# SwiGLU by block products: three pairs in units 1 to 7 instead of two, six pairs in each of two passes of the last product, and SiLU as one ScalarE step

## The chip, the cores and the metric

The kernel is one program on one core of a Trainium2 chip. The core has five engines that run side by side: TensorE (PE in the profile; its weight loads are listed as PEld), VectorE (DVE), ScalarE (ACT), GpSimd (POOL) and SyncE (SP), which here only issues DMAs. The metric is the device time of one execution in microseconds; lower is better.

## What is computed

The reference is one transformer block on 256 tokens of width 2048, all in fp32. A conditioning vector gives six modulation vectors (`w_ada`), a mixing sublayer of three branches follows, and then a SwiGLU feed-forward part, which is the part that matters here:

```
def swiglu(h, w_ffn_in, w_ffn_out):
    gate, up = jnp.split(h @ w_ffn_in, 2, axis=-1)
    return (jax.nn.silu(gate) * up) @ w_ffn_out

h = rms_norm(x, norm2_gain[l]) * (1 + scale2) + shift2
x = x + gate2 * swiglu(h, w_ffn_in[l], w_ffn_out[l])
```

`h` is 256 x 2048, `w_ffn_in` is 2048 x 11264 (gate and up, 5632 columns each), `w_ffn_out` is 5632 x 2048. The results must come out at fp32 quality.

## The kernel before

**Products in three parts.** TensorE multiplies in fp32r. Each fp32 operand is split into a high part (the value rounded to fp32r) and a low part (the remainder), and a product is three matmuls: high by high, high by low, low by high (`mm3`, lines 158 to 161). The stationary operand is a 128x128 block of the transposed activations, the moving one 128 rows x 512 columns of weights; the sum goes into a PSUM bank of 128 x 512. There are eight banks in two pools of four, `acc` and `misc`.

**Weights.** A DMA on SyncE's queue brings 2 blocks of 128 x 512 into a buffer `raw` (four of these, 512 KB each). ScalarE casts it to `whi`, VectorE subtracts `whi` from `raw` into `wlo`. There are four buffers of each, and I call one `whi` with its `wlo` a slot. In `load_weights` these are lines 153 and 154, in `load_pair` lines 1266 and 1267. A slot can be cast again only when TensorE has read it for the last time, and a `raw` buffer can be loaded again only when its last reader on VectorE or ScalarE is done. All engines, and SyncE's queue, work strictly in order. The order on each engine is set when the program is built, by a scheduler that goes by priorities; loads and evictions run at raised priority.

**SwiGLU, first product.** 5632 columns are 11 units (`i` of 0 to 10) of 512 gate and 512 up columns. A plain unit is 16 blocks of the contraction x 2 row halves (tokens 0 to 127 and 128 to 255) x 2 column blocks x 3 matmuls, 192 in all. Units 1 to 7 go through `fast_unit`. It takes the contraction in eight pairs of blocks (`PAIRS`), and a pair with the two row halves and two column blocks (gate and up) is a 2x2 by 2x2 product of blocks. A plain pair does its 8 block products, 24 matmuls, and needs two slots. A pair marked 1 is done by seven block products (Strassen's scheme in Winograd's form), 21 matmuls: VectorE forms four sums of weight blocks (line 1270, into the buffers `OD` and `KD`), the weights then fill four slots (one of them half), and four sums of activation blocks (`sums_of_h2`) are made once, in unit 0. Products that are needed in more than one output go into four banks of the other pool; after the last such pair VectorE adds them up (line 1294: four steps that form the combinations, and four that add them into the unit's own banks, while plain pairs still run). Pairs 6 and 7 are fast, in the order 0, 1, **6**, 2, **7**, 3, 4, 5.

After a unit ScalarE takes the sigmoid of the gate half (line 1361), VectorE multiplies by the gate (line 1362) and by the up half (line 1373), and behind the first pair of the next unit TensorE transposes the result (line 1110: eight transposes), which is split into high and low parts (lines 186, 187).

**A background task.** The modulation vector `gate2` is computed on VectorE in pieces placed by `tick` between the other work (line 283: 32 steps of one weight block times one scalar; loads into `AR0`, `AR1`, `KC`). It starts at unit 8 and ends in the first pass of the last product with four bias rows (line 966) and eight short steps that go from ScalarE (line 975) to VectorE (976) to TensorE (980, 981) through one buffer `T6`; `flush` places whatever is left.

**SwiGLU, last product.** Four passes `n` of 512 output columns, each 44 blocks of the contraction x 2 row halves x 3 matmuls. Each pass ends with `add_out` (times `gate2`, plus the residual, store). In the last pass the final 14 blocks are loaded ahead and the row halves run one after the other, so that little is left behind the last matmul.

Of the kernel before, what the change touches and what calls it, by code (L numbers as in the profile page):

```python
# [71 lines left out]
def trunk(ctx: ExitStack, tc: tile.TileContext, I, out):  # L72
# [15 lines left out]
    def S(tag, shape, dtype=F32):  # L88
        return slot.tile(shape, dtype, tag=tag, name=nm(tag))
# [1090 lines left out]
    def norm2_turn(t, xs):  # L1180
        c = slice(t * P, (t + 1) * P)
        banks = []
        for j in range(KC // 4):
            ps = misc_bank([P, 4, P])
            for i in range(4):
                k = 4 * j + i
                nc.tensor.transpose(ps[:, i, :], xs[:, k * P : (k + 1) * P], ident)
            banks.append(ps)
        for j, ps in enumerate(banks):
            hf = S(f"T6", [P, 4, P]) if (j, t) == (3, 0) else scr([P, 4, P])  # L1190
            if j == 3:
                h2_raw.append(hf)
# [9 lines left out]
    h2_raw = []  # L1202
# [38 lines left out]
    def sums_of_h2():  # L1241

        sf = S("KC", [P, 4, 2, P])
        (a0, b0), (a1, b1) = ((h[:, 0:4:2, :], h[:, 1:4:2, :]) for h in h2_raw)
        for dst, x, y, op in (
            (0, a1, b1, ALU.add), (2, a0, a1, ALU.subtract), (1, sf[:, 0], a0, ALU.subtract), (3, b0, sf[:, 1], ALU.subtract)
        ):
            nc.vector.tensor_tensor(sf[:, dst], x, y, op=op)
        hi, lo = S("OS1", [P, 4, 2, P], F32R), S("OS2", [P, 4, 2, P], F32R)
        nc.scalar.copy(hi, sf)  # L1250
        nc.vector.tensor_tensor(lo, sf, hi.bitcast(F32), op=ALU.subtract)
        return hi, lo

    def load_pair(p, c0, c1, fast):


        def raw_at(c):
            raw = wp.tile([P, 2, NB], F32, tag="raw", name=nm("raw"))
            nc.sync.dma_start(raw, w_ff[2 * p * P : (2 * p + 2) * P, c : c + NB].rearrange("(k p) c -> p k c", p=P))
            return raw  # L1260

        def split(src):
# [8 lines left out]
        with prio():  # L1271
            if not fast:
                return [split(raw_at(c0)), split(raw_at(c1))]
            r0, r1 = raw_at(c0), raw_at(c1)
            b11, b21 = split(r0)
            ta, tb = S("OD", [P, 2, NB]), S("KD", [P, 2, NB])
# [9 lines left out]
    def fast_unit(i):  # L1286


        own, other = (misc_bank, acc_bank) if i % 2 else (acc_bank, misc_bank)
        ws = [load_pair(p, i * NB, DFF + i * NB, fast) for p, fast in PAIRS]  # L1290
        o = [[own([P, NB]) for _ in range(NT)] for _ in range(2)]
        shared = []
        last_fast = max(n for n, (_, fast) in enumerate(PAIRS) if fast)
        add = lambda dst, x, y: nc.vector.tensor_tensor(dst, x, y, op=ALU.add)
        for n, ((p, fast), w) in enumerate(zip(PAIRS, ws)):
            tick(2 * state["rate"])
            if n == 1 and later:
                with tc.issue_after(state["mm"].ins), prio():
                    later.pop()()
            if n == last_fast + 2:  # L1300
                with prio():
                    add(o[0][0], o[0][0], first)
                    add(o[1][0], o[1][0], u[:, 1])
            if n == last_fast + 3:
                with prio():
                    add(o[0][1], o[0][1], third)
                    add(o[1][1], o[1][1], u[:, 0])
            begun, merged = n > 0, n > last_fast
            if fast:
                if not shared:  # L1310
                    shared = [other([P, NB]) for _ in range(4)]
                    p1, p5, p7, p6 = shared
                    begun = False
                else:
                    begun = True
                s = [(h2s[0][:, j, p - 6, :], h2s[1][:, j, p - 6, :]) for j in range(4)]
                a, b = 2 * p, 2 * p + 1
                lefts = (h2_at(a, 0), h2_at(b, 0), s[3], s[0], s[2], s[1], h2_at(b, 1))
                for dst, (h, l), (wh, wl) in zip((p1, o[0][0], o[1][0], p5, p7, p6, o[0][1]), lefts, w):
                    mine = dst in shared  # L1320
                    mm3(dst, h, l, wh, wl, mine and not begun, n == last_fast, False)
            else:
                for c in range(2):
                    for t in range(NT):
                        for k in range(2):
                            h, l = h2_at(2 * p + k, t)
                            mm3(o[c][t], h, l, *w[c][k], not begun and k == 0,
                                k == 1 and (n == len(PAIRS) - 1 or n > last_fast or (c, t) == (1, 1) and n == last_fast - 1), n > last_fast)
            if n == last_fast:
                with prio():  # L1330
                    u, first, third = S("KC", [P, 2, NB]), S("T6", [P, NB]), scr([P, NB])
                    nc.scalar.copy(first, p1)
                    add(u[:, 0], p6, first)
                    add(u[:, 1], p5, u[:, 0])
                    add(third, p7, u[:, 0])
                    add(u[:, 0], p5, third)
        return o

    state["rate"] = RATE_FFN
    ring["tags"] = ("AR0", "AR1", "KC")  # L1340
    act = []
    for i in range(NFF):
# [11 lines left out]
                block(pg, h2_at, None, 0, KC, 0, w=w, tiles=(t,), steps=None if t else {N2_AT[1]: lambda: norm2_turn(1, xs)})  # L1354
        else:
            block(pg, h2_at, w_ff, 0, KC, i * NB)
        sgs = []
        with prio():
            for t in range(NT):
                sg = scr([P, NB])  # L1360
                nc.scalar.activation(sg, pg[t], AF.Sigmoid)
                nc.vector.tensor_mul(sg, sg, pg[t])
                sgs.append(sg)
        if i == 0:
            h2s = sums_of_h2()
# [31 lines left out]
    KF = 4 * NFF  # L1397
    CUT = KF - 14
    w_fo = I["w_ffn_out"]
    for n in range(4):  # L1400
        pss = [acc_bank() for _ in range(NT)]
        if n == 3:

            block(pss, act_at, w_fo, 0, CUT, n * NB, more=True)
            w = load_weights(w_fo, CUT, KF, n * NB, spare=[f"H{j}" for j in range(2, 8)])
            block(pss, act_at, None, CUT, KF, 0, w=w, tiles=(0,), go_on=True)
            with prio():
                add_out(n, 0, pss[0])

            block(pss, act_at, None, CUT, KF - LASTK, 0, w=w, tiles=(1,), go_on=True, more=True)  # L1410
            side = acc_bank()
            for cols, ps in ((slice(0, NB - LASTC), pss[1][:, : NB - LASTC]), (slice(NB - LASTC, NB), side[:, :LASTC])):
                for k in range(KF - LASTK, KF):
                    wh, wl = w[k - CUT]
                    h, l = act_at(k, 1)
                    mm3(ps, h, l, wh[:, cols], wl[:, cols], k == KF - LASTK and cols.start > 0, k == KF - 1)
                if cols.start == 0:
                    add_out(n, 1, pss[1], end=NB - LASTC)
                    add_out(n, 1, pss[1], NB - LASTC, store=False)
            add_out(n, 1, side, NB - LASTC, base=NB - LASTC)  # L1420
        else:
            if n == 0:
                state["rate"] = RATE_OUT
            block(pss, act_at, w_fo, 0, KF, n * NB)
            if n == 0:
                flush()
                gate2 = state["gate2"]
            with prio():
                for t in range(NT):
                    add_out(n, t, pss[t])  # L1430


_INS = ["x", "c", "w_ada", "b_ada", "norm1_gain", "norm2_gain", "w_in", "sb_q_gain", "sb_k_gain", "dil_q_gain",
# [23 lines left out]
```

## Time and profile before

| | |
|---|---|
| median of 3 runs | 1604.01 us (1603.54 to 1604.73) |
| the profiled execution | 1603.22 us, of which 1601.4 us span from the first to the last instruction |
| granted TensorE clock | 1.00 in that execution |
| first product, units 0 to 10 | about 882 to 1359 us of the span |
| last product | about 1359 to 1601 us |

The profile gives busy time per engine, tables of busy time by stretch of the span, groups of instructions by line, a list of instructions in order of time, a chain of work that ended last, and the waits with what ended each. An instruction's row has its start, its duration and, in brackets, the idle time ahead of it on its engine with what ended that. A row with xN merges N instructions that followed each other.

### The profile page before, as it was taken

What the parts mean: (1) busy time and instruction counts of PE and PEld (TensorE: products, weight loads), DVE (VectorE), ACT (ScalarE), POOL (GpSimd) and SP (SyncE); (2) the same over time, 40 slices, a digit from 0 to 9 for tenths busy, and PEclk for the clock granted to TensorE, in tenths of its full rate; (3) what the DMA queues carried; (4) which work ended last, traced back from release to release, by engine and by line L of the source; (5) the groups of instructions that cost most, each with busy time, mean ns of one, the idle gap of its engine ahead of it and who ended that gap; (6) DMA issues with size and microseconds to landing.
All of it is one profiled execution on the core that took longest, in us unless ns stands there. A gap on an engine that the chain in (4) does not pass through costs nothing.

```text
span 1601.4 us, 20082 instructions
## 1 busy us (share of the span) xinstructions
PE 1589.3 (99%) x7308; PEld 1314.7 (82%) x7308; DVE 1207.8 (75%) x1417; ACT 814.6 (51%) x1155; POOL 5.3 (0%) x14
## 2 busy tenths in 40 slices
PE   8999999999999999999999999999999999999998
PEld 7878888888888888888887888888888888878887
DVE  6889996888877787878657688888887777474453
ACT  5654449775754434444446555555544444444332
POOL 1000000000000000000000000000000000000000
PEclk9999999999999999999999999999999999999999
DMA  9999997668778899898666566655567799666663
GB/s 332 361 327 323 331 305 246 214 184 261 247 254 288 300 302 309 300 312 299 224 192 194 167 194 194 197 193 182 189 209 235 260 313 307 224 209 193 202 206 110
DMA packets 194595, 395.96 MB, mean 247 GB/s; under 512 B 12914, under 2 KB 27928, under 8 KB 194496
## 3 DMA queue, kind: packets, MB, share of 16 engines
q1 hardware_dynamic: 194096, 394.60, 74.9%
q8 instruction: 57, 0.93, 0.2%
q14 instruction: 42, 0.34, 0.1%
q10 hardware_dynamic: 176, 0.07, 0.0%
q0 software_dynamic: 224, 0.01, 0.0%
HBM read 392.53 MB, written 2.10 MB: 246 GB/s over the span
## 4 chain that ended last, share of the span: by engine, by line
PE 90%; DVE 3%; ACT 3%; DMA 3%; issue 1%; SPq 0%; ACTq 0%; DVEq 0%
PE acc L161 24%; PE acc L160 24%; PE acc L159 24%; PE misc L159 4%; PE misc L161 4%; PE misc L160 4%; DVE wlo L154 1%; DMA raw<-w_in 1%; ACT whi L153 1%; PE acc L429 1%; PE misc L795 1%; PE misc L1110 1%; ACT scr L624 1%; DMA A<-x 0%; DMA raw<-w_br_gla 0%
## 5 line engine op out<-in xcount | busy, mean ns | idle before, releaser
L154 DVE TENSOR_TENSOR wlo<-raw,whi 128x1024 fp32r<-128x1024 f32 (+1 forms) x434 | 514.4, 1191 | 280.3 <-ACT whi L153 278.2
L153 ACT CAST whi<-raw 128x1024 fp32r<-128x1024 f32 (+1 forms) x434 | 444.0, 1026 | 529.1 <-PE acc L161 384.2
L159 PE MATMUL acc<-whi,H 128*128 128x512 f32 x1292 | 505.7, 392 | 1.4 <-ACT H L441 0.8
L160 PE MATMUL acc<-wlo,H 128*128 128x512 f32 x1292 | 504.6, 391 | 0.8 <-DVE wlo L154 0.7
L161 PE MATMUL acc<-whi,H 128*128 128x512 f32 x1292 | 503.5, 390 | 0.4 <-DVE H L448 0.4
L161 PEld LDWEIGHTS acc<-whi,H 128*128 128x128 f32 x1292 | 242.4, 188 | 52.3 <-DVE H L448 1.6
L159 PEld LDWEIGHTS acc<-whi,H 128*128 128x128 f32 x1292 | 242.5, 188 | 52.0 <-ACT H L441 1.3
L160 PEld LDWEIGHTS acc<-wlo,H 128*128 128x128 f32 x1292 | 242.7, 188 | 50.7 <-DVE wlo L154 1.7
L1266 ACT CAST whi<-raw 128x1024 fp32r<-128x1024 f32 x112 | 109.9, 998 | 86.6 <-PE acc L161 37.4
L1267 DVE TENSOR_TENSOR wlo<-raw,whi 128x1024 fp32r<-128x1024 f32 x112 | 125.8, 1155 | 12.4 <-ACT whi L1266 12.1
L160 PE MATMUL acc<-wlo,A 128*128 128x512 f32 x312 | 121.6, 390 | 0.4 <-DVE wlo L154 0.4
L159 PE MATMUL acc<-whi,A 128*128 128x512 f32 x312 | 122.0, 391 | 0.0
L161 PE MATMUL acc<-whi,A 128*128 128x512 f32 x280 | 109.1, 390 | 0.0
L159 PE MATMUL misc<-whi,H 128*128 128x512 f32 x214 | 83.6, 391 | 0.0
L161 PE MATMUL misc<-whi,H 128*128 128x512 f32 x214 | 83.3, 389 | 0.0
L160 PE MATMUL misc<-wlo,H 128*128 128x512 f32 x214 | 83.3, 389 | 0.0
L283 DVE SCALAR_TENSOR_TENSOR ada<-AR,csil,ada 128x1024 f32<-128x1024 f32 x59 | 74.9, 1280 | 3.5 <-DMA AR<-w_ada 3.4
L160 PEld LDWEIGHTS acc<-wlo,A 128*128 128x128 f32 x312 | 58.6, 188 | 12.6 <-DVE wlo L154 0.8
L159 PEld LDWEIGHTS acc<-whi,A 128*128 128x128 f32 x312 | 58.6, 188 | 11.8
L161 PEld LDWEIGHTS acc<-whi,A 128*128 128x128 f32 x280 | 52.6, 188 | 10.6
L161 PE MATMUL acc<-whi,OS 128*128 128x512 f32 x142 | 55.3, 389 | 0.0
L161 PEld LDWEIGHTS misc<-whi,H 128*128 128x128 f32 x214 | 40.2, 188 | 8.4
(396 smaller groups left out, 1761.4 us busy)
## 6 DMA issues: line engine op xcount, KB each, us to landing
raw<-w_in SPq DMA_DIRECT2D x205, 512.0 KB, 5.1
raw<-w_ffn_in SPq DMA_DIRECT2D x176, 512.0 KB, 4.4
raw<-w_ffn_out SPq DMA_DIRECT2D x88, 512.0 KB, 4.6
AR<-w_ada SPq DMA_DIRECT2D x79, 512.0 KB, 5.0
raw<-w_out SPq DMA_DIRECT2D x32, 512.0 KB, 3.8
KC<-w_ada SPq DMA_DIRECT2D x30, 512.0 KB, 5.2
OS<-w_ada SPq DMA_DIRECT2D x16, 512.0 KB, 6.4
KD<-w_ada SPq DMA_DIRECT2D x16, 512.0 KB, 4.7
```

Of the source, the lines that this page charges most:

```text
L153: state["cast"] = nc.scalar.copy(hi[:, :n, :], raw[:, :n, :])
L154: state["split"] = nc.vector.tensor_tensor(lo[:, :n, :], raw[:, :n, :], hi[:, :n, :].bitcast(F32), op=ALU.subtract)
L159: nc.tensor.matmul(ps, lh, rh, start=start, stop=False, skip_group_check=seeded)
L160: nc.tensor.matmul(ps, lh, rl, start=False, stop=False, skip_group_check=seeded)
L161: state["mm"] = nc.tensor.matmul(ps, ll, rh, start=False, stop=stop, skip_group_check=seeded)
L283: nc.vector.scalar_tensor_tensor(acc, raw, c, acc, op0=ALU.mult, op1=ALU.add)
L429: state["warm"] = nc.tensor.matmul(ps, ones_r, wide, start=True, stop=True)
L624: nc.scalar.activation(junk, heads(b)[:, t, h, :], AF.Square, accum_out=ss[:, t, i : i + 1])
L795: nc.tensor.matmul(ps[:n, t * N_GLA + h, :].rearrange("p (s l) -> p s l", l=L), at(f, h, t)[:, :n], odd(at(f, h, t)), start=True, stop=True,)
L1110: nc.tensor.transpose(ps[:, i, :], src[:, i * P : (i + 1) * P], ident)
L1266: nc.scalar.copy(hi[:, :n, :], src)
L1267: state["split"] = nc.vector.tensor_tensor(lo[:, :n, :], src, hi[:, :n, :].bitcast(F32), op=ALU.subtract)
```

## The change

1. `PAIRS`: in units 1 to 7 pairs 5, 6 and 7 are fast, in the order 0, 1, **5**, 2, **6**, **7**, 3, 4. The merge of the shared products, formerly before the seventh and eighth pair, comes before the eighth pair and after it. `sums_of_h2` makes the activation sums of pair 5 as well (kept in `AR0`) and stands before the first SiLU.
2. The last product goes through the same function in two passes of two column blocks each. Pass A (columns 0 to 1023) has 22 pairs: 7 plain, then six times a fast and a plain one, then 3 plain. Pass B (columns 1024 to 2047) has two plain pairs and six times a fast and a plain one; the remaining 16 blocks then run as before, one column block after the other. The fast pairs are those of units 4, 5 and 6 (pairs 8 to 13); their activation sums are made in pass A from high plus low part (`sums_of_unit`, before pairs 1, 2 and 4 of the order), in `AR0`, `AR1` and `H2` to `H7`. Weight sums use `AR0` and `AR1`. In pass A the loads are issued three pairs ahead (`LOOK`), and the background task must be finished before the first fast pair (`hooks[7] = flush`).
3. Sigmoid and the multiplication by the gate become one `Silu` on ScalarE.

```
-RATE_OUT = 2.0
+RATE_OUT = 2.5
+LOOK = 3
-PAIRS = ((0, 0), (1, 0), (6, 1), (2, 0), (7, 1), (3, 0), (4, 0), (5, 0))
+OUT_UNITS = (4, 5, 6)
+OUT_A = tuple((p, 0) for p in range(7)) + tuple(x for i in range(6) for x in ((8 + i, 1), ((7, 14, 15, 16, 17, 18)[i], 0))) + (
+    (19, 0), (20, 0), (21, 0))
+OUT_B = ((0, 0), (1, 0)) + tuple(x for i in range(6) for x in ((8 + i, 1), (2 + i, 0)))
+PAIRS = ((0, 0), (1, 0), (5, 1), (2, 0), (6, 1), (7, 1), (3, 0), (4, 0))
...
+    def fast_products(src, c0, c1, order, at, sums, own, other, tags, hooks={}, more=False):
...
+        load(LOOK if hooks else len(order))
...
+        for n, (p, fast) in enumerate(order):
             tick(2 * state["rate"])
+            if n in hooks:
+                hooks[n]()
+            load(n + LOOK)
...
+            for half in range(2):
+                if n == last_fast + 2 + half:
+                    merge(half)
...
+        for half in range(2):
+            if end <= last_fast + 2 + half:
+                merge(half)
         return o
...
-                nc.scalar.activation(sg, pg[t], AF.Sigmoid)
-                nc.vector.tensor_mul(sg, sg, pg[t])
+                nc.scalar.activation(sg, pg[t], AF.Silu)
...
+    def sums_of_unit(n):
+
+        e = OUT_UNITS[n]
+        full = S("AR0", [P, 4, T])
+        nc.vector.tensor_tensor(full, act[e][0].bitcast(F32), act[e][1].bitcast(F32), op=ALU.add)
+        sf = S("AR1", [P, 4, 2, P])
+        sums_of(sf, [full[:, :, t * P : (t + 1) * P] for t in range(NT)], slice(0, 4, 2), slice(1, 4, 2))
+        hi, lo = (S(f"H{2 + 2 * n + i}", [P, 4, 2, P], F32R) for i in range(2))
+        nc.scalar.copy(hi, sf)
+        nc.vector.tensor_tensor(lo, sf, hi.bitcast(F32), op=ALU.subtract)
...
+    hooks = {at: (lambda n=n: sums_of_unit(n)) for n, at in enumerate((1, 2, 4))}
+    hooks[7] = flush
+    o = fast_products(w_fo, 0, NB, OUT_A, act_at, out_sums, acc_bank, misc_bank, ("AR0", "AR1"), hooks)
...
+    o = fast_products(w_fo, 2 * NB, 3 * NB, OUT_B, act_at, out_sums, misc_bank, acc_bank, ("AR0", "AR1"), more=True)
+    REST = 2 * len(OUT_B)
+    block(o[0], act_at, w_fo, REST, KF, 2 * NB, go_on=True, seeded=True)
```

More of the change, by code (lines that the diff above doesn't have):

```diff
@@ L1284, in load_pair, with load, merge @@
             return b11, b21, b22, t1, t3, t2, t4
-    def fast_unit(i):
-        own, other = (misc_bank, acc_bank) if i % 2 else (acc_bank, misc_bank)
-        ws = [load_pair(p, i * NB, DFF + i * NB, fast) for p, fast in PAIRS]
+    def fast_products(src, c0, c1, order, at, sums, own, other, tags, hooks={}, more=False):
+        ws = []
+        def load(n):
+            while len(ws) < min(n, len(order)):
+                ws.append(load_pair(src, order[len(ws)][0], c0, c1, order[len(ws)][1], tags))
+        load(LOOK if hooks else len(order))
         o = [[own([P, NB]) for _ in range(NT)] for _ in range(2)]
         shared = []
-        last_fast = max(n for n, (_, fast) in enumerate(PAIRS) if fast)
-        add = lambda dst, x, y: nc.vector.tensor_tensor(dst, x, y, op=ALU.add)
-        for n, ((p, fast), w) in enumerate(zip(PAIRS, ws)):
+        end = len(order)
+        first_fast, last_fast = (f(n for n, (_, fast) in enumerate(order) if fast) for f in (min, max))
+        last_plain = max(n for n in range(last_fast) if not order[n][1])
+        add = lambda dst, x: nc.vector.tensor_tensor(dst, dst, x, op=ALU.add)
+        def merge(half):
+            with prio():
+                add(o[0][half], (first, third)[half])
+                add(o[1][half], u[:, 1 - half])
+        for n, (p, fast) in enumerate(order):
             tick(2 * state["rate"])
+            if n in hooks:
+                hooks[n]()
+            load(n + LOOK)
+            w = ws[n]
             if n == 1 and later:
@@ L1299, in fast_unit @@
                     later.pop()()
[L1300 to L1308, printed above, removed]
+            for half in range(2):
+                if n == last_fast + 2 + half:
+                    merge(half)
+            merged = n > last_fast
             if fast:
@@ L1399, in trunk @@
     w_fo = I["w_ffn_out"]
[L1400 to L1430, printed above, removed]
@@ new lines, in trunk @@
+    REST = 2 * len(OUT_B)
+    block(o[0], act_at, w_fo, REST, KF, 2 * NB, go_on=True, seeded=True)
+    with prio():
+        for t in range(NT):
+            add_out(2, t, o[0][t])
+    n, pss = 3, o[1]
+    block(pss, act_at, w_fo, REST, CUT, n * NB, go_on=True, more=True, seeded=True)
+    w = load_weights(w_fo, CUT, KF, n * NB, spare=[f"H{j}" for j in range(2, 8)])
+    block(pss, act_at, None, CUT, KF, 0, w=w, tiles=(0,), go_on=True, seeded=True)
+    with prio():
+        add_out(n, 0, pss[0])
@@ new lines, in trunk @@
+    block(pss, act_at, None, CUT, KF - LASTK, 0, w=w, tiles=(1,), go_on=True, more=True, seeded=True)
+    side = acc_bank()
+    for cols, ps in ((slice(0, NB - LASTC), pss[1][:, : NB - LASTC]), (slice(NB - LASTC, NB), side[:, :LASTC])):
+        for k in range(KF - LASTK, KF):
+            wh, wl = w[k - CUT]
+            h, l = act_at(k, 1)
+            mm3(ps, h, l, wh[:, cols], wl[:, cols], k == KF - LASTK and cols.start > 0, k == KF - 1, cols.start == 0)
+        if cols.start == 0:
+            add_out(n, 1, pss[1], end=NB - LASTC)
+            add_out(n, 1, pss[1], NB - LASTC, store=False)
```

73 lines of the change are left out of this document (46 added, 27 removed).

## The prediction

> **What bounds the kernel now.** I read the page's first part, then the table of stretches, the chain, and then two units in order of time on VectorE and ScalarE. First the page, and stretches: a fast unit, a plain unit, the start of the last product (columns: TensorE, weight loads, VectorE, ScalarE, GpSimd, granted clock, DMA share, GB/s).
>
> ```profile
> PE 1589.3 (99%) x7308; PEld 1314.7 (82%) x7308; DVE 1207.8 (75%) x1417; ACT 814.6 (51%) x1155; POOL 5.3 (0%) x14
> ...
> 1053.19:1096.26 43.07, 43.07 (x196) 35.74 (x195) 36.18 (x43) 22.35 (x25) 0.00 (x0) 1.00 0.62 197
> 1225.46:1269.89 44.43, 44.43 (x202) 36.86 (x201) 30.40 (x29) 18.89 (x20) 0.00 (x0) 1.00 0.78 253
> 1358.74:1422.00 63.26, 63.26 (x284) 51.94 (x283) 38.12 (x37) 26.66 (x30) 0.00 (x0) 1.00 0.71 226
> ```
>
> TensorE has no idle time in any of the three, at full clock. Here a matmul less is time less, as long as VectorE (36.18 of 43.07 us in a fast unit) keeps up. The chain of work shows the unit's period, by its transposes:
>
> ```profile
> 1182.39 0.87 PE acc L1110 x8
> 1225.46 0.88 PE misc L1110 x8
> 1269.89 0.87 PE misc L1110 x8
> ```
>
> A fast unit (186 matmuls and the transposes) takes 43.07 us, a plain one (192) 44.43. So six matmuls are 1.36 us, one is 0.227, a block product of three is 0.68.
>
> **The gain.** Each pair done by seven products instead of eight saves 0.68 us. Units 1 to 7 get one more each, the last product 12: 19 x 0.68 = 12.9 us (57 matmuls; the built program has 57 fewer on TensorE). [...]
>
> **What it costs on VectorE.** How densely VectorE and ScalarE work:
>
> ```profile
> 1059.23 0.69 DVE L1270 TENSOR_TENSOR OD<-raw,raw 128x512 f32<-128x512 f32 x1
> 1059.84 0.68 DVE L1270 TENSOR_TENSOR OD<-raw 128x512 f32<-128x512 f32 x1
> ...
> 1068.13 1.22 DVE L1267 TENSOR_TENSOR wlo<-OD,whi 128x1024 fp32r<-128x1024 f32 x1 [0.87 <-ACT whi L1266]
> 1070.89 1.23 DVE L1267 TENSOR_TENSOR wlo<-KD,whi 128x1024 fp32r<-128x1024 f32 x1 [1.54 <-ACT whi L1266]
> 1072.33 4.63 DVE L1267 TENSOR_TENSOR wlo<-raw,whi 128x1024 fp32r<-128x1024 f32 x4 [0.21 <-ACT whi L1266]
> ```
>
> ```profile
> 1067.05 1.05 ACT L1266 CAST whi<-OD 128x1024 fp32r<-128x1024 f32 x1 [2.10 <-PE acc L161]
> 1069.81 1.05 ACT L1266 CAST whi<-KD 128x1024 fp32r<-128x1024 f32 x1 [1.71 <-PE acc L161]
> 1070.77 0.58 ACT L1332 COPY T<-misc 128x512 f32<-128x512 f32 x1
> 1071.24 2.98 ACT L1266 CAST whi<-raw 128x1024 fp32r<-128x1024 f32 x3
> ```
>
> In a full queue starts are 0.60 us apart (512 columns) and (4.63-1.23)/3 = 1.14 (1024), although one lasts 0.69 and 1.22. ScalarE's casts are (2.98-1.05)/2 = 0.96 apart, and a `wlo` starts 1.08 after the start of its cast (1069.81 to 1070.89). A plain pair needs two `wlo`, 2.28 us of VectorE; a fast one three and a half `wlo` and four weight sums, 3 x 1.14 + 5 x 0.60 = 6.42. Removed in each unit are the two multiplications of line 1362:
>
> ```profile
> L1362 DVE TENSOR_TENSOR scr<-scr,acc 128x512 f32<-128x512 f32 x14 | 9.4, 684 | 2.2 <-ACT scr L1361 2.2
> L1361 ACT ACTIVATE scr<-acc 128x512 f32<-128x512 f32 x14 | 8.4, 598 | 6.4 <-PE acc L161 6.2
> L1332 ACT COPY T<-acc 128x512 f32<-128x512 f32 x4 | 2.3, 578 | 0.0
> L812 ACT ACTIVATE T<-T 128x512 f32<-128x512 f32 x8 | 5.2, 644 | 4.3 <-DVE T L821 4.2
> ```
>
> That is 1.2 us less per unit, and nothing on TensorE's path, since TensorE never waits for it. No row shows a Silu of 512 columns; the nearest are the copy's 0.58 and the 0.64 of line 812, and I take the sigmoid's 0.60. [...] The built order has as many table loads as before (4).
>
> *Units 1 to 7.* VectorE's load becomes 36.18 + 4.14 - 1.20 = 39.1 us of a unit that should shrink to 43.07 - 0.68 = 42.4; ScalarE's grows by 1.5. The average fits; the narrow place is where fast pairs 6 and 7 follow each other, with 2 x 4.76 = 9.5 us of matmuls against 12.8 us of VectorE. I walked VectorE's built order through one unit, T from its first matmul. A plain slot is read for 2.72 us, those of a fast pair for 1.36, 0.68, 1.36, 1.36, and the transposes (0.88) follow the first pair. Pair 5 then starts at 11.76, pair 2 at 16.52, pair 6 at 21.96, pair 7 at 26.72, pair 3 at 31.48. A slot is cast once the slot four before it has been read (the casts of 1067.05 and 1069.81 come 0.06 and 0.10 after that). Pair 7's weight sums start when its second `raw` lands: the buffer is freed by pair 2's second `wlo` (16.0 to 17.2), and a load takes this:
>
> ```profile
> raw<-w_ffn_in SPq DMA_DIRECT2D x112, 512.0 KB, 4.4
> ```
>
> So they run from 21.75 to 22.95. Pair 6's last `wlo` must wait for its slot (cast 22.06, `wlo` 23.14, done 24.4; read at 25.6). After it VectorE works without a gap: a sum to 25.0, pair 7's first `wlo` to 26.2 (read at 26.95), second to 26.7, a sum to 27.3, third 27.3 to 28.5 (read at 28.99), fourth to 29.8 (read at 30.35), pair 3's first to 30.9 (read at 31.7). The smallest margin is 0.4 us. The chain of eight merge steps and the next unit's first slots (done at 41.4, wanted at 42.4) fit as well. So the walk gives no stall; against landings up to 0.6 us late it holds. I allow 0.4 us for all seven units (ends 0 and 7 x 0.7 = 4.9, where a unit saves nothing).
>
> *Unit 0.* The sums for pair 5 are four steps of 128 columns, a cast and a `wlo` of 512: 2.5 us of VectorE at most, 1.2 removed, behind four slots already filled. Zero. `AR0` now stays occupied to unit 7, so `gate2`'s first two loads, made early before, come later; VectorE has room in units 8 to 10 (30.40 of 44.43). Zero.
>
> *Start of pass A.* Here the cover runs out. Before, this stretch had 38.12 us of VectorE in 63.26. Now the rest of `gate2` and the activation sums stand ahead of the first fast pair, 40.5 us behind the pass's start. Prices from these rows:
>
> ```profile
> 889.81 0.42 DVE L1248 TENSOR_TENSOR KC<-T,scr 128x256 f32<-128x256 f32 x1
> 890.16 0.43 DVE L1248 TENSOR_TENSOR KC<-scr 128x256 f32<-128x256 f32 x1
> 890.62 0.43 DVE L1248 TENSOR_TENSOR KC<-KC,T 128x256 f32<-128x256 f32 x1
> ...
> 1405.43 1.28 DVE L283 SCALAR_TENSOR_TENSOR ada<-KC,csil,ada 128x1024 f32<-128x1024 f32 x1
> 1406.63 1.28 DVE L283 SCALAR_TENSOR_TENSOR ada<-AR,csil,ada 128x1024 f32<-128x1024 f32 x1
> ...
> 1413.80 1.88 DVE L966 TENSOR_TENSOR ada<-ada,scr 1x512 f32<-1x512 f32 x3
> ...
> 1416.74 0.41 DVE L976 TENSOR_TENSOR T<-ada,T 128x256 fp32r<-128x256 f32 x1
> 1417.08 0.67 DVE L966 TENSOR_TENSOR ada<-ada,scr 1x512 f32<-1x512 f32 x1
> ```
>
> VectorE's built order from the pass's start to the fast pair's last `wlo` holds 14 `wlo` of 1024 (16.0), five steps of line 283 (6.0), eight additions and their splits for three units (6 x 1.14 + 12 x 0.41 = 11.7), four bias rows (2.4), eight steps of line 976 (2.8), two multiplications, two transposed splits, four weight sums and a half `wlo` (9 x 0.60 = 5.4): 44.3 us, and 2.5 of waiting for slots and transposes early on, so that it ends at about 47. TensorE wants that `wlo` at 44.6: 2.4 us late. The next fast pair's first load waits for the weight sums just made (44.4), lands 4.8 us later, and ScalarE casts it ahead of the copy that frees the last `gate2` bank. That bank takes the shared product that TensorE has next, at about 50.7; in all some 3.9 us late. From there each fast and plain pair asks 8.7 us of VectorE in 10.2 of TensorE, so nothing is added. Lower end 0 (the order fills the gaps), upper end 8 (a landing like the slowest here, 7.1, and two more waits in a row):
>
> ```profile
> DMA to landing us min/median/max: 4.4/4.8/7.1
> ```
>
> *Merges and pass B.* The shared products of pass A are merged while three plain pairs run (walked: done 1 us before each bank is written again). Behind pass B's last fast pair only 5.4 us of matmuls cover the merge of column block 2's banks, which takes 0.6 + 6 x 0.60 + a 1.14; walked, the second bank is ready at 10.25 against 10.9. Zero, at most 1. The tail behind the last matmul is unchanged.
>
> **Sum.** 12.9 - 0.4 - 3.9 = 8.6 us saved. The profiled execution's own 1603.22 (span 1601.4 and 1.8 around it) becomes 1594.6; it lies 0.8 under the median, so I predict 1595.4 for the median. Its own range is 1592.5 to 1599.
>
> **Rivals.**
> 1. *All of it is hidden.* The scheduler puts other products where TensorE would wait. For it: the walk has only 2.4 us at the first place. Against: the bank. 12.9 us gained, 1591.1.
> 2. *VectorE becomes the bound.* If dependent steps start only when the one before is done, each costs 0.09 more: 46 steps in a unit make 39.1 into 43.2 us, above 42.4, 7 x 0.8 = 5.6 lost, and 70 steps at pass A's start lose 6 more. 12.9 - 5.6 - 9.9 = a loss of 2.6 at its full size, 1606.6; half of it gives 1601. For it: 890.62 follows 890.16 by 0.46, where 890.16, which reads nothing of 889.81, follows it by 0.35. Against: the four steps in 4.63 us. [...]
> 3. *Slower: late landings before pair 7.* Each us by which its second `raw` comes more than 0.6 late stops TensorE as long, in seven units. To lose all of 8.6 and 3.2 more takes 1.7 us a unit, a landing of 6.7 instead of 4.4: 1607.5. For it: the 7.1 above, in a stretch at 0.71 of DMA time. Against: 0.62 in the fast units, whose DMA grows by nothing.
>
> **Chances.** Forecast 0.50, rival 1 0.15, rival 2 0.27 (spread over 1599 to 1607), rival 3 0.08. A change under 0.2%, 3.2 us, is not told from none here. Faster (under 1600.8): 0.50 + 0.15 + 0.15 = 0.80; the same: 0.12 of rival 2; slower 0.08. The range 1590.5 to 1602 leaves out rival 3, the upper part of rival 2 and little else.
>
> **What would show it.** Right: a fast unit's period by its transposes near 42.4 us with TensorE without idle time and VectorE near 39; at pass A's start, about 40 to 50 us behind its first matmul, idle time of TensorE of 3 to 5 us, ended by VectorE's `wlo` and by ScalarE's copy of a `gate2` bank; from there on a fast and a plain pair every 10.2 us. Wrong: a period above 42.8 us with waits on `wlo` in pair 7 (rival 2, or 3 if the weight sums wait for `raw`), no idle time at pass A's start (rival 1), or waits at pass B's merge.

## The result and the profile after

The changed kernel takes 1599.72 us (median; 1598.42 to 1600.58) against 1603.78 us of the kernel before on the same chip: a ratio of 0.9969, 95% interval 0.9958 to 0.9979. That is 4.1 us less, where the matmuls left out are worth 12.9 and I had forecast 8.6. The profiled execution took 1599.73 us with a span of 1597.9. About 9 us were lost somewhere, and the question is where.

First the page's line of engines, then, in a fence of its own, the table of stretches (columns as in the prediction): a fast unit, the interval from unit 10's transposes to those that stand in pass A, and what follows them.

```profile
PE 1583.3 (99%) x7251; PEld 1304.2 (82%) x7251; DVE 1289.7 (81%) x1548; ACT 849.7 (53%) x1199; POOL 5.4 (0%) x14
```

```profile
1051.92:1095.16 43.24, 43.14 (x192) 34.94 (x191) 38.68 (x48) 24.03 (x27) 0.00 (x0) 1.00 0.58 195
...
1313.97:1362.02 48.05, 46.25 (x202) 37.87 (x200) 34.62 (x31) 18.91 (x20) 0.00 (x0) 0.97 0.87 298
1362.02:1425.00 62.98, 62.33 (x278) 49.68 (x277) 57.86 (x74) 35.28 (x45) 0.00 (x0) 1.00 0.60 191
```

VectorE's load in a fast unit is 38.68 us, as foreseen (39.1), but the unit takes 43.24, hardly more than the 43.07 of before. The interval of 48.05 was a plain 44.43 before, and its granted clock is 0.97. The transposes of units 1 and 8 (TensorE's list in order of time) stand this far apart, first in the kernel before and then in the changed one:

```profile
923.83 0.27 PE L1110 MATMUL acc<-ident,scr 128*128 128x128 f32 x1
...
1225.29 0.28 PE L1110 MATMUL misc<-ident,scr 128*128 128x128 f32 x1
```

```profile
923.41 0.27 PE L1115 MATMUL acc<-ident,scr 128*128 128x128 f32 x1
...
1225.12 0.28 PE L1115 MATMUL misc<-ident,scr 128*128 128x128 f32 x1
```

Seven units took 301.46 us and take 301.71. With six matmuls less they should have become 301.46 - 4.76 = 296.70. So the books are:

| where | lost, us | forecast, us |
|---|---|---|
| units 1 to 7: 301.71 - 296.70 | 5.0 | 0.4 |
| unit 10's transposes to pass A's: 48.05 - 44.43 | 3.6 | 0 |
| from there to the end of the span: 235.88, where before took 242.83 and 12 block products are 8.16 | 1.2 | 3.9 |
| sum | 9.8 | 4.3 |

12.9 - 9.8 = 3.1 us, and another 0.4 lies ahead of unit 1 (923.83 against 923.41); the spans differ by 3.5. The 0.4 says nothing: over all the traces of this case that point lies anywhere from 923.0 to 926.3. The 5.0 is one execution's too: in the profiles of the four runs below whose units are exactly those of the changed kernel (`units_only`, `rate_late`, `mul_first`, `later_fast`), the seven take 300.0 to 301.0 us, 3.3 to 4.3 lost.

**Where a fast unit stops.** TensorE and then VectorE in unit 4, whose first matmul starts at 1046.48 (5.44 ahead of its transposes), and SyncE's queue:

```profile
1073.34 0.39 PE L164 MATMUL misc<-whi,H 128*128 128x512 f32 x1
1073.83 0.50 PE L165 MATMUL misc<-wlo,H 128*128 128x512 f32 x1
...
1075.79 0.40 PE L164 MATMUL misc<-whi,OS 128*128 128x512 f32 x1
1076.17 0.50 PE L165 MATMUL misc<-wlo,OS 128*128 128x512 f32 x1
```

```profile
1069.48 0.69 DVE L1286 TENSOR_TENSOR OD<-raw,raw 128x512 f32<-128x512 f32 x1 [1.11 <-DMA raw<-w_ffn_in]
1070.09 0.68 DVE L1286 TENSOR_TENSOR OD<-raw 128x512 f32<-128x512 f32 x1
1070.69 1.22 DVE L1283 TENSOR_TENSOR wlo<-KD,whi 128x1024 fp32r<-128x1024 f32 x1
1071.95 0.69 DVE L1286 TENSOR_TENSOR KD<-raw,OD 128x512 f32<-128x512 f32 x1
1072.56 1.82 DVE L1283 TENSOR_TENSOR wlo<-raw,whi 128x1024 fp32r<-128x1024 f32 x2
```

```profile
1064.34 0.37 SPq L1275 DMA_DIRECT2D raw<-w_ffn_in  x1
```

The matmuls that read `wlo` in pair 7 (line 165) come 0.49 and 0.38 us behind their neighbours instead of 0.23. VectorE makes that `wlo` at 1072.56, because pair 7's weight sums begin at 1069.48, when the second `raw` lands, and VectorE has stood idle for 1.11 us by then. The load was issued at 1064.34 and took 5.1 us.

**What happens at pass A's start.** TensorE, then VectorE, and the granted clock behind the wait:

```profile
1355.45 0.39 PE L166 MATMUL acc<-whi,A 128*128 128x512 f32 x1
1357.64 0.47 PE L164 MATMUL acc<-whi,A 128*128 128x512 f32 x1 [1.80 <-DVE scr L1404]
...
1359.03 0.63 PE L166 MATMUL acc<-whi,A 128*128 128x512 f32 x1
1359.46 0.63 PE L164 MATMUL acc<-whi,A 128*128 128x512 f32 x1
```

```profile
1354.47 1.28 DVE L288 SCALAR_TENSOR_TENSOR ada<-AR,csil,ada 128x1024 f32<-128x1024 f32 x1 [1.83 <-DMA AR<-w_ada]
1355.67 1.22 DVE L1283 TENSOR_TENSOR wlo<-raw,whi 128x1024 fp32r<-128x1024 f32 x1
1356.81 1.28 DVE L1404 TENSOR_TENSOR scr<-scr,acc 128x512 f32<-128x512 f32 x2
```

```profile
1358.60:1362.00 3.40, 3.40 (x9) 2.53 (x8) 2.96 (x3) 0.76 (x1) 0.00 (x0) 0.51 0.97 301
```

Pass A's first pair needs four `acc` banks at once. Two of them still hold unit 10's up half, and the two multiplications that free them (line 1404) stand on VectorE behind a step of the background task that waits 1.83 us for its load. TensorE waits 1.80 us, and behind that its matmuls are 0.43 us apart instead of 0.23 for 3.4 us, at a granted clock of 0.51. The same order stood in the kernel before:

```profile
1353.45 1.28 DVE L283 SCALAR_TENSOR_TENSOR ada<-AR,csil,ada 128x1024 f32<-128x1024 f32 x1 [0.89 <-DMA AR<-w_ada]
...
1355.79 1.28 DVE L1373 TENSOR_TENSOR scr<-scr,acc 128x512 f32<-128x512 f32 x2
```

But there the pass took two banks, both long free, and TensorE did not wait. The change was therefore not only in what is computed: the pass's need of banks doubled, and a wait that had been harmless was now on the path.

### The profile page after: what moved, and what is told of

Read it like the earlier page. It is cut to its first block, busy times and chain, and to the rows that moved or that the text cites. A ratio compares the mean times of both kernels' runs of the same rounds, so it can differ in the third digit from the quotient of the medians.

```text
span 1597.9 us, 20173 instructions
## 1 busy us (share of the span) xinstructions
PE 1583.3 (99%) x7251; PEld 1304.2 (82%) x7251; DVE 1289.7 (81%) x1548; ACT 849.7 (53%) x1199; POOL 5.4 (0%) x14
## 4 chain that ended last, share of the span: by engine, by line
PE 78%; DVE 9%; DMA 6%; ACT 4%; issue 2%; SPq 0%; DVEq 0%; ACTq 0%
PE acc L165 20%; PE acc L166 20%; PE acc L164 20%; PE misc L165 5%; PE misc L166 5%; PE misc L164 5%; DMA raw<-w_ffn_in 4%; DVE wlo L1283 3%; ACT whi L158 1%; DVE wlo L159 1%; DVE OD L1286 1%; DMA AR<-w_ada 1%; DMA raw<-w_br_gla 1%; PE acc L434 1%; DVE KD L1286 1%
## 5 line engine op out<-in xcount | busy, mean ns | idle before, releaser
L158 ACT CAST whi<-raw 128x1024 fp32r<-128x1024 f32 x362 | 368.7, 1022 | 417.2 <-PE acc L166 266.3
L159 DVE TENSOR_TENSOR wlo<-raw,whi 128x1024 fp32r<-128x1024 f32 x362 | 425.6, 1183 | 188.0 <-ACT whi L158 185.8
L1282 ACT CAST whi<-raw 128x1024 fp32r<-128x1024 f32 (+1 forms) x184 | 175.7, 974 | 114.1 <-PE acc L166 50.3
L1283 DVE TENSOR_TENSOR wlo<-raw,whi 128x1024 fp32r<-128x1024 f32 (+1 forms) x184 | 200.3, 1123 | 13.3 <-ACT whi L1282 12.3
L164 PE MATMUL acc<-whi,A 128*128 128x512 f32 x222 | 87.5, 396 | 2.3 <-DVE scr L1404 1.8
L165 PE MATMUL acc<-wlo,A 128*128 128x512 f32 x222 | 87.4, 394 | 0.4 <-DVE wlo L159 0.4
L166 PE MATMUL acc<-whi,A 128*128 128x512 f32 x216 | 85.0, 393 | 0.0
L164 PEld LDWEIGHTS acc<-whi,A 128*128 128x128 f32 x222 | 41.9, 189 | 11.7 <-issue 2.2
L165 PEld LDWEIGHTS misc<-wlo,H 128*128 128x128 f32 x225 | 42.2, 188 | 10.6 <-DVE wlo L1283 1.9
L164 PEld LDWEIGHTS misc<-whi,H 128*128 128x128 f32 x225 | 42.2, 188 | 9.4 <-ACT whi L1282 0.7
L165 PEld LDWEIGHTS acc<-wlo,A 128*128 128x128 f32 x222 | 42.0, 189 | 9.4 <-DVE wlo L159 0.8
L166 PEld LDWEIGHTS misc<-whi,H 128*128 128x128 f32 x225 | 42.2, 188 | 8.6
```

The source lines that it names most:

```text
L158: state["cast"] = nc.scalar.copy(hi[:, :n, :], raw[:, :n, :])
L159: state["split"] = nc.vector.tensor_tensor(lo[:, :n, :], raw[:, :n, :], hi[:, :n, :].bitcast(F32), op=ALU.subtract)
L164: nc.tensor.matmul(ps, lh, rh, start=start, stop=False, skip_group_check=seeded)
L165: nc.tensor.matmul(ps, lh, rl, start=False, stop=False, skip_group_check=seeded)
L166: state["mm"] = nc.tensor.matmul(ps, ll, rh, start=False, stop=stop, skip_group_check=seeded)
L1282: nc.scalar.copy(hi[:, :n, :], src)
```

## Experiments

All times are medians; each ratio is to the kernel before on the same chip.

**The two halves apart.** `units_only` joins the first product of the changed kernel to the old last product; `last_only` keeps the old `PAIRS`.

> Three fast pairs in units 1 to 7 and the Silu, with the last product of the kernel before (four passes, rate 2.0). It saves 7 x 0.68 = 4.8 us of matmuls. Theory 'late raw' (pair 7's weight sums start when its second raw lands, late in every unit, whatever follows): the units' periods stay those of the changed kernel, 42.5 to 43.8 us, 301.7 us for the seven against 301.5 before, so the time is that of before within 1 us, about 1603.5 to 1604.5. Rival (the units lose only what the forecast allowed, 0.4 us, and the rest was lost elsewhere): 4.4 us less, about 1599.4.

Measured: 1603.38 us, ratio 0.9996 (0.9987 to 1.0005). The seven units take 300.0 us here, 1.5 of the 4.8 less than before.

> The last product in two passes with six fast pairs each and the Silu; the units keep the two fast pairs of before. It saves 12 x 0.68 = 8.2 us of matmuls. Theory (pass A loses about 4.6 us at its start: the wait for unit 10's bank of 1.9, half clock behind it 1.6, the first fast pair 1): 8.2 - 4.6 = 3.6 us less than before, about 1600.2, with the same interval of 48 us from unit 10's transposes to pass A's. Rival (those waits come from what the third pair pushes on: the later start of the background task): nothing of it, 8.2 less the 1 of the fast pair, about 1596.6.

Measured: 1600.71 us, ratio 0.9981 (0.9971 to 0.9991). The third fast pair brought no gain clear of the noise (1.5 us in the units' trace); most of what the change gained came from the last product. Pass A's bank wait is there without the third pair too (1.71 us in its trace), so the third pair did not cause it. But its matmuls stayed at 0.23 us, so the interval to pass A's transposes is 46.42 us, not the 48 that I expected, and from there to the end 237.62 us pass, 2.9 more than the 234.67 left of before without 12 block products: waits at gate2's row matmuls and the first fast pair. The expectation had the sum, not its parts.

**A buffer of its own for the late `raw`.**

```
-            r0, r1 = raw_at(c0), raw_at(c1)
+            r0, r1 = raw_at(c0), raw_at(c1, own_raw.get(p) if src is w_ff else None)
```

(`own_raw` is `{7: "AR1"}`; with a tag, `raw_at` takes that buffer.)

> The changed kernel, with one edit: in units 1 to 7 the second raw of pair 7 is loaded into AR1, which is free there, instead of into the ring of four; it can then be loaded before pair 2's second wlo is done. Theory 'late raw': pair 7's weight sums no longer wait, the units come to about 42.5 us, 4 to 5 us less in all, about 1595.2. Rival 'VectorE bound' (its dependent steps are too slow, whenever the weights land): no change, 1599.7. In between if pair 6's raw, which comes late too, is what counts: 1597 to 1598.

Measured: 1595.55 us, ratio 0.9949 (0.9935 to 0.9963). First the same unit in the table of stretches, then the waits of units 1 to 7 from the tables of waits of the changed kernel and of this one (us in total, times, longest):

```profile
1051.93:1094.32 42.39, 42.39 (x192) 35.18 (x191) 38.79 (x48) 23.95 (x27) 0.00 (x0) 1.00 0.60 198
```

```profile
DVE OD L1286 <- DMA raw<-w_ffn_in: 10.9, 14, 1.3
PEld misc L165 <- DVE wlo L1283: 3.4, 8, 0.6
```

```profile
DVE OD L1288 <- DMA raw<-w_ffn_in: 4.1, 6, 0.8
PEld misc L165 <- DVE wlo L1285: 0.4, 2, 0.2
```

With the same work on VectorE (38.79 us) the unit comes to the 42.39 us of its matmuls, without idle time. Pair 7's weight sums begin 21.8 us behind the unit's first matmul, where the walk had 21.75. So VectorE was not short of time; it was kept from using it. The loads of `raw` still take a median of 5.0 us to land: what helped is that the late one no longer waits for a buffer of the ring. Pass A's wait for the bank stayed (1.55 us, at full clock).

**The SiLU.** `silu_only` is the kernel before with `AF.Silu` alone, `sigmoid` the changed kernel with

```
-                nc.scalar.activation(sg, pg[t], AF.Silu)
+                nc.scalar.activation(sg, pg[t], AF.Sigmoid)
+                nc.vector.tensor_mul(sg, sg, pg[t])
```

> The kernel before, with SiLU as one step of ScalarE and nothing else changed: 1.2 us less of VectorE in each of 11 units, the same matmuls. Theory (before the change TensorE never waits for VectorE in the units, so its work there is free): no change, 1603 to 1605, periods 43.07 and 44.43 us. Rival (VectorE's load is on the path): up to 1.2 us less in each unit, 1591 at the full size and 1600 at a third of it.

Measured: 1604.88 us, ratio 1.0003 (0.9994 to 1.0013).

> The changed kernel, with SiLU as before (sigmoid on ScalarE, a multiplication on VectorE: 1.2 us more of VectorE in each of 11 units). Theory (what holds TensorE in the units is the landing of pair 7's raw, and VectorE has idle time around the unit's end, where the multiplications stand): within 1 us, 1599 to 1600.7. Rival 'VectorE bound': 7 x 1.2 = 8.4 us more at the most, 1604 at half of it.

Measured: 1598.07 us, ratio 0.9958 (0.9942 to 0.9974). More work on VectorE, and not slower; the median is even 1.6 us lower than the changed kernel's and 0.9 below what I expected, though the two intervals of ratios overlap. A fast unit in the table of stretches, and VectorE in order of time at the start of pass A:

```profile
1053.29:1096.40 43.11, 43.04 (x192) 34.97 (x191) 39.57 (x49) 23.90 (x27) 0.00 (x0) 1.00 0.61 195
```

```profile
1352.34 1.29 DVE L288 SCALAR_TENSOR_TENSOR ada<-AR,csil,ada 128x1024 f32<-128x1024 f32 x1 [0.82 <-DMA AR<-w_ada]
...
1354.68 1.28 DVE L1405 TENSOR_TENSOR scr<-scr,acc 128x512 f32<-128x512 f32 x2
```

The unit's period is that of the changed kernel with 0.9 us more on VectorE. The difference sits at pass A: here the background step's load kept VectorE waiting for 0.82 us instead of 1.83, the multiplications came 2 us earlier against TensorE, and there was no wait for the bank; behind it 2.5 us were lost instead of 1.2. I read this as an accident of when one load lands, not as a merit of the sigmoid; no run separates the two.

**The start of pass A: more background work early.** From unit 8 on `RATE_FFN` is replaced by 0.85.

> The changed kernel, with one edit: from unit 8 on the background task is placed at 0.85 steps instead of 0.65 for every two blocks, so that all its 32 multiply-and-add steps stand ahead of unit 10's two last multiplications and none waits for a late load right before them. Theory (TensorE waits for unit 10's bank because such a step, waiting for its load, stands ahead of the multiplications on VectorE; behind the idle time the clock is half for 3.4 us): wait and half clock go, 3.6 us, and the start of pass A has less of VectorE, so up to 1 us at the first fast pair: 1595.1 to 1596.1. Rival (pass A takes four banks at once, and the multiplications are late in any order): at most 1 us less, 1598.7 to 1599.7.

Measured: 1606.66 us, ratio 1.0015 (1.0006 to 1.0024): slower than both kernels. The bank's wait is gone as expected, but units 9 and 10 now take 48.72 and 53.22 us to the next transposes. SyncE's queue, ScalarE and TensorE in unit 9:

```profile
1295.22 0.33 SPq L376 DMA_DIRECT2D KC<-w_ada  x1
1295.60 10.62 SPq L147 DMA_DIRECT2D raw<-w_ffn_in  x7
...
1300.82 1.04 ACT L159 CAST whi<-raw 128x1024 fp32r<-128x1024 f32 x1 [4.55 <-DMA raw<-w_ffn_in]
...
1301.92 0.50 PE L165 MATMUL acc<-whi,H 128*128 128x512 f32 x1 [1.36 <-ACT whi L159]
1303.18 0.50 PE L166 MATMUL acc<-wlo,H 128*128 128x512 f32 x1 [0.76 <-DVE wlo L160]
```

Seven loads of weights stand behind background loads in one queue, the last of them issued at 1295.22; ScalarE then waits 4.55 us for the first, and TensorE stops. I had counted the extra steps' time on VectorE, not the place of their loads in the queue. The run says nothing on the bank but that the wait can be removed.

**The start of pass A: the multiplications first.**

```
-            if (k - k0) % 2 == 0 and tiles[-1] == NT - 1:
+            if (k - k0) % 2 == 0 and tiles[-1] == NT - 1 and not (c0 == 2 * DFF - NB and k >= 8):
...
-            tick(2 * state["rate"])
+            if n or not hooks:
+                tick(2 * state["rate"])
```

> The changed kernel, with one edit: no piece of the background task is placed in the second half of unit 10's up block and in pass A's first pair. That moves two of its steps (and their loads) from ahead of unit 10's two last multiplications to behind pass A's first weights; the total is the same. Theory (TensorE waits 1.8 us for unit 10's bank because a step that waits for its load stands ahead of the multiplications; the half clock for 3.4 us follows from that wait): no wait at pass A's bank, no slow matmuls behind it, unit 10's interval from 48.05 to 44.5 us; the two steps of 1.2 us now stand in VectorE's dense stretch and come back at the first fast pair, 0 to 2.4 us: 1596.2 to 1598.6. Rival (loads of w_ffn_out are what is late there, and any order waits): the interval stays above 47 us and the time at 1599.7 or above.

Measured: 1604.69 us, ratio 1.0002 (0.9992 to 1.0012).

> The two edits together: pair 7's second raw of units 1 to 7 in AR1, and no background step in the second half of unit 10's up block and pass A's first pair. If the two losses are separate, the gains add: 1595.5 measured with the first alone, less a bank wait of 1.9 (its clock did not fall there), plus 0 to 2.4 at the first fast pair: 1593.6 to 1596. Rival: the steps held back cost more than the bank wait (above 1596).

Measured: 1600.67 us, ratio 0.9980 (0.9970 to 0.9989). Each of the two runs came out 5 us worse than the same kernel without this edit, against my expectation. The bank's wait is gone (unit 10 takes 44.41 us in `both`), and the units are at 42.4 there, but 40 us further on, at the first fast pair of pass A, TensorE in `both` does this (in order of time, and the stretch around it):

```profile
1394.41 0.39 PE L985 MATMUL misc<-T,ones_r 128*128 128x256 f32 x1 [1.05 <-ACT T L980]
1395.65 0.39 PE L986 MATMUL misc<-T,ones_r 128*128 128x256 f32 x1 [0.85 <-DVE T L981]
1396.53 0.38 PE L985 MATMUL misc<-T,ones_r 128*128 128x256 f32 x1 [0.49 <-ACT T L980]
1398.32 0.58 PE L986 MATMUL misc<-T,ones_r 128*128 128x256 f32 x1 [1.41 <-DVE T L981]
```

```profile
1391.86:1404.62 12.76, 8.30 (x21) 5.35 (x20) 10.62 (x16) 7.37 (x11) 0.00 (x0) 0.73 0.39 122
```

All of `gate2` must be finished ahead of the first fast pair, and its last matmuls (lines 985, 986) wait one by one for ScalarE and VectorE, which hand a single buffer `T6` to and fro. TensorE is busy for 8.30 of 12.76 us, and the clock falls again. From pass A's transposes to the end `both` needs 244.5 us, where `raw_own`, which lacks only this edit, needs 236.7: two steps of 1.2 us, moved behind the multiplications, cost 7.8 us there and saved the 1.8 of the bank's wait. My range of 0 to 2.4 took them as time on VectorE, but they are the head of a chain over three engines.

**Cover for that chain.** The edit of `mul_first`, and two of the plain pairs at pass A's end stand ahead of its first fast pair:

```
-OUT_A = tuple((p, 0) for p in range(7)) + tuple(...) + ((19, 0), (20, 0), (21, 0))
+OUT_A = tuple((p, 0) for p in (0, 1, 2, 3, 4, 5, 6, 19, 20)) + tuple(...) + ((21, 0),)
...
-    hooks[7] = flush
+    hooks[9] = flush
```

> The changed kernel, with the edit of mul_first (no background step in the second half of unit 10's up block and pass A's first pair) and one more: two of the three plain pairs at pass A's end (19 and 20 of the contraction) go ahead of its first fast pair, and the background task must be finished two pairs later. Theory (what the start of pass A loses is either the wait for unit 10's bank or, if the steps are pushed back, the wait of TensorE's row matmuls of gate2, which must all stand ahead of the first fast pair; 10.9 us more of plain matmuls cover both): no waits from unit 10 to pass A's first fast pair, 4 us less than the changed kernel, 1595 to 1596.5. Rival (with one plain pair left behind the last fast pair of pass A the merge is late, or the row matmuls wait anyway): 1598 or above.

Measured: 1595.30 us, ratio 0.9944 (0.9932 to 0.9956).

> The edits of raw_own and later_fast together: pair 7's second raw of units 1 to 7 in AR1, the background steps behind unit 10's multiplications, two plain pairs more ahead of pass A's first fast pair. If the units' late raw and the start of pass A are all that the change lost, nearly the whole 12.9 us stay: 1591 to 1592.5. Rival (losses hidden so far come up, at the merges or in pass B): 1594 or above.

Measured: 1592.01 us, ratio 0.9924 (0.9910 to 0.9937). A fast unit of `best`, and the stretch behind pass A's transposes:

```profile
1051.34:1093.71 42.37, 42.37 (x193) 35.17 (x191) 38.70 (x48) 24.01 (x27) 0.00 (x0) 1.00 0.62 199
1354.21:1417.00 62.79, 62.40 (x280) 49.62 (x279) 58.13 (x72) 34.03 (x43) 0.00 (x0) 1.00 0.64 209
```

Both losses are gone with the same matmuls and the same work on every engine (VectorE 1289.6 us against 1289.7). 12 of the 12.9 us stay, and the two causes add up: 1599.7 with neither edit, 1595.6 with the buffer, 1595.3 with the order, 1592.0 with both.

**Another order of pairs in the units.** `PAIRS` as 0, 1, 5, 2, 6, 3, 7, 4.

> The changed kernel, with one edit: the order of pairs in units 1 to 7 is 0, 1, 5, 2, 6, 3, 7, 4 (5, 6, 7 fast), so that a plain pair stands between fast pairs 6 and 7, and the merge of the shared products begins behind pair 7 with one plain pair left. Theory 'late raw': pair 7's second raw is wanted 5.4 us later, the units come to 42.5 us, 1595 (as with the buffer of its own). Rival: the merge, now with 5.4 us less before the unit's end, is late for SiLU and for the transposes of the next unit, and gives 0.5 us or more a unit back: 1598.5 or above.

Measured: 1607.64 us, ratio 1.0021 (1.0010 to 1.0031). Loads land earlier again (median 4.5 us in units 1 to 7), and pair 7 no longer stops TensorE, but the units take 43.2 to 44.9 us. The wait is now near the first fast pair of a unit (VectorE, then TensorE):

```profile
1021.88 0.69 DVE L1286 TENSOR_TENSOR OD<-raw,raw 128x512 f32<-128x512 f32 x1 [1.94 <-DMA raw<-w_ffn_in]
1022.50 3.49 DVE L1283 TENSOR_TENSOR wlo<-raw,whi 128x1024 fp32r<-128x1024 f32 x3
...
1023.77 0.50 PE L165 MATMUL misc<-wlo,H 128*128 128x512 f32 x1 [1.46 <-DVE wlo L1283]
```

The rival had the size (more than 0.5 us a unit given back) but not the place: a weight sum of the next fast pair waits 1.94 us for its load, and three `wlo` that TensorE wants stand behind it. Whether the later merge or the new order of loads makes that load late was not separated. The theory's 1595 fell with it: moving the late `raw` by a plain pair only moves the wait.

**What idle time does to the clock.** `best` with four additions that nobody reads among unit 10's last multiplications.

> The kernel of best with four extra additions of 512 columns on VectorE (their result is not used) among unit 10's two last multiplications, so that pass A's bank comes about 2.4 us later, and nothing else is late. It asks what TensorE's clock does behind an idle time of its own making. If an idle time of 1.8 us or more brings the half clock (1.80 did in the changed kernel, 1.71 and 1.55 did not in two others): a wait of 1.5 to 2.5 us and, if it is over 1.8, matmuls at 0.43 us for 3.4 us behind it. If the half clock of the changed kernel had another cause: the wait alone, matmuls at 0.23 behind it.

Measured: 1601.36 us in a single run. TensorE at the bank, and at the first row matmul of gate2:

```profile
1357.97 0.50 PE L164 MATMUL acc<-whi,A 128*128 128x512 f32 x1 [1.43 <-DVE scr L1412]
1358.31 0.40 PE L165 MATMUL acc<-wlo,A 128*128 128x512 f32 x1
...
1387.69 0.58 PE L985 MATMUL misc<-T,ones_r 128*128 128x256 f32 x1 [2.00 <-ACT T L980]
...
1390.63 0.59 PE L166 MATMUL acc<-whi,A 128*128 128x512 f32 x1
1391.06 0.39 PE L164 MATMUL acc<-whi,A 128*128 128x512 f32 x1
```

A wait of 1.43 us leaves the matmuls as fast as they were; one of 2.00 us brings 0.43 us a matmul for the 3.4 us to 1391.06. I was wrong that nothing else would be late: from unit 10's transposes to the end this execution takes 288.1 us, that of `best` 279.7. So 2.4 us more on VectorE came back as 8.4, at the bank and through the same chain as in `both`, with the clock at half in two stretches of 3.4 us. (The two profiled executions differ by 10.0 us; the other 1.6 lie ahead of unit 1, where runs scatter.)

## Why the prediction came out as it did

The sign and the range were right; the time of 4.1 us less lies between my forecast of 8.6 and nothing, above the likeliest case's own range (1592.5 to 1599). That range was narrower than the ends that I had named for the two places: 4.9 and 8 us lost would have left nothing of the 12.9.

- *The gain*, 19 x 0.68 = 12.9 us, holds: `best` realises 12.1 of it, and a fast unit without waits takes 42.37 to 42.39 us (forecast 42.4).
- *VectorE's load in a unit*, 39.1 us: 38.68 measured. The step prices held: the rows of unit 4 follow each other by 0.61, 0.60 and 0.61 us.
- *The walk of a fast unit* is the step that failed, at the 4.4 us for a landing and at the moment the buffer is freed. I had pair 7's weight sums at 21.75 us behind the unit's first matmul, good for 0.6 us more. They begin at 1069.48 - 1046.48 = 23.0, 1.25 late: the load is issued at 17.9, where I had 17.2, and lands 5.1 us later instead of 4.4 to 4.5. The tolerance was sound (1.25 - 0.6 is 0.65 us; that unit lost 0.85), the 0.4 us allowed for seven units were not; they lost 5.0 in this execution, at the upper end that I had named, 4.9, "where a unit saves nothing". The landings of `raw` in units 1 to 7, before and after:

```profile
DMA to landing us min/median/max: 3.5/4.4/5.5
```

```profile
DMA to landing us min/median/max: 3.6/5.0/5.6
```

  I had taken a median of the old rhythm of loads for the new one. In `apart`, whose fast pairs stand apart, the median is 4.5. That adjacent fast pairs bunch the loads fits this; what makes a bunched load slower was not measured.
- *Pass A's start*: 3.9 us forecast, 3.6 + 1.2 = 4.8 lost, but mostly by another mechanism. The step "Merges and pass B" looked at banks inside and behind the passes and not at the first pair, which wants four `acc` banks while two are unread. The one I forecast, late VectorE work ahead of the first fast pair and gate2's chain, is real: it cost 1.2 us here, 2.5 where the bank did not hold TensorE up (`sigmoid`), and 7.8 more when 2.4 us of steps came on top (`both`). TensorE's stop at the bank gave VectorE time to catch up, so the two losses do not simply add, and the forecast's 3.9 was near the sum by luck. In part TensorE waited elsewhere than I had put it: at the row matmuls of gate2 (lines 985, 986), which I had counted only as VectorE's steps; the rest came at the first fast pair, as forecast.
- *Merges and the rest of the last product*: no loss forecast, none found. TensorE has no listed wait behind 1405 us of the changed kernel's trace.
- *The clock* was in no step: 1.6 of the 3.6 us (eight matmuls at 0.43) in the profiled execution, whose mean clock is 0.999. Of the six executions two have 1.000, so it did not fall in each.
- *Rival 1* (all hidden) is what `best` shows to be possible, not what happened. *Rival 2* (VectorE the bound): refuted by `raw_own`, by `sigmoid`, where 0.9 us more in a unit changed no period, and by `silu_only`. The rows of unit 4, 0.60 and 0.61 us apart at 0.69 us each, are of steps that read nothing of the one just before, and they start ahead of its end. Where a step reads it (line 1286, 1052.61 behind 1051.89), the starts are 0.72 us apart: the rival's extra price was there, but not in every step. *Rival 3* (late landings before pair 7) was the right mechanism, and 0.08 was too little for it: it took all of the units' 4.8 us without turning the sign, since it has no effect on the last product. What I had held against it came true and did not help: the DMA share in a fast unit did not grow (0.58 against 0.62), and the landings were slower all the same. (Its time should read 1607.2, 1595.4 + 11.8.)
- *SiLU* at no gain and 0.60 us: right (the 14 Silu steps of the changed kernel, line 1395, have a mean of 599 ns; `silu_only` 1.0003).

## What to carry to other kernels

When work per unit of time shrinks on the bounding engine, walk the loads and banks again with the new rhythm: here a buffer ring that had been just long enough and banks that had been free came up short (5.0 and 3.6 us lost there), while VectorE's load (38.7 of 42.4 us) still looked comfortable. VectorE took its steps in the order built, so one that waited 1.83 us for its own load cost what stood behind it, two multiplications and through them 1.80 us of TensorE. Give the late item its own buffer or more cover behind it: the two edits took 7.7 us (1599.7 to 1592.0) without removing any work.

## What was not expected of the hardware

TensorE's granted clock fell to half (0.51 over 3.40 us in the changed kernel) behind an idle time of 1.80 us. Single waits of 1.43 (`idle_test`), 1.55 (`raw_own`) and 1.71 us (`last_only`) left it at full speed; 1.80 (the changed kernel) and 2.00 us (`idle_test`) brought 3.4 us at half speed, starting up to 1 us behind the wait. Behind waits of 1.36 and 0.76 us close together (`rate_late`) the matmuls from 1304.46 on are 0.43 us apart, and with four between 0.5 and 1.4 us in 5 us (`both`) the granted clock is 0.73 over 12.76 us. A fall cost the changed kernel 1.6 us on top of the wait.

The length of a wait does not decide it alone, though. In unit 7 of `apart` TensorE waited 2.01 us and went on at full clock, 15 matmuls in the next 3.40 us where the changed kernel had 9 behind its wait:

```profile
1199.88 0.50 PE L165 MATMUL misc<-wlo,H 128*128 128x512 f32 x1 [2.01 <-DVE wlo L1283]
```

```profile
1199.90:1203.30 3.40, 3.40 (x15) 2.83 (x16) 3.40 (x5) 0.49 (x1) 0.00 (x0) 1.00 0.66 192
```

And in `idle_test` the clock fell a second time, from 1411.54 to 1414.95, where the waits listed just ahead were 0.32 and 0.49 us. The half speed (in the changed kernel matmuls 0.43 us apart instead of 0.23) lasted 3.4 us there and both times in `idle_test`. What does decide it stays open: no limit on the length of a single wait fits these rows.
